# Experts' weights in whole rows over two PSUM banks, with the halves of neighbouring experts interleaved

## The chip, the core and the metric

The kernel runs on one core of a Trainium2 chip. The metric is device time in microseconds (us) from the first to the last instruction of one launch, as the median of several runs. Engines are named as the profile names them: PE multiplies matrices and PEld loads its stationary operand, ACT and DVE work on elements, POOL issues gathers and scatters, SP issues the loads of the weights. The products accumulate in PSUM, which has eight banks of 128 x 512 fp32 here.

## What is computed

Two transformer blocks over 1024 tokens of 1024 channels. The change lies in the experts of the first block. Each of 16 experts takes the 128 tokens that it prefers (twice the 1024 tokens over 16 experts); its three weights have 1024 x 1024 elements in fp32.

```python
def ec_moe(x_tok, w_router, w_gate, w_up, w_down):
    t = x_tok.shape[1]
    cap = CAP_FACTOR * t // N_EXPERTS
    logits = jnp.einsum('btd,de->bte', x_tok, w_router, preferred_element_type=jnp.float32)
    aff = jax.nn.softmax(logits, axis=-1)
    g, idx = lax.top_k(jnp.swapaxes(aff, 1, 2), cap)
    xs = jax.vmap(lambda xt, ix: xt[ix])(x_tok, idx)
    hg = jnp.einsum('becd,edf->becf', xs, w_gate)
    hu = jnp.einsum('becd,edf->becf', xs, w_up)
    y = jnp.einsum('becf,efd->becd', jax.nn.silu(hg) * hu, w_down) * g[..., None].astype(xs.dtype)
    return jax.vmap(lambda ix, val: jnp.zeros((t, D_MODEL), val.dtype)
                    .at[ix.reshape(-1)].add(val.reshape(-1, D_MODEL)))(idx, y)
```

Ahead of the experts stands a mixer of attention and convolution, behind them a second block (`block2`, `final`); neither is touched.

## The kernel before

Every fp32 product is made in three passes. `split` writes an operand as a high part (an ACT cast to fp32r, L82) and a low part (a DVE subtraction, L83), and `mm3` adds high by high, high by low and low by high in one PSUM bank (L77, L78, L79). For a block of weights the parts are `whi` and `wlo`.

The experts run one after another (`moe`, `expert`). For one expert POOL gathers its tokens into `xs` [128 tokens, 1024]; PE transposes them in eight 128 x 128 pieces through two PSUM tiles `tp` (L677), and ACT and DVE split these into `xsh` and `xsl`. Then, for each half `n` of the 1024 columns, `pg` takes the gate product and `pu` the up product; ACT makes `sl = silu(pg)` (L703) and DVE `hh = sl * pu` (L704). The whole `hh` is transposed as `xs` was and split into `hth` and `htl`, which multiply the down weights; the result stands in a tile that is also called `pg`, ACT scales it by the gate into `y` (L711), and POOL scatters `y` with addition into `ff_d` (L712).

The weights come in 192 blocks of 1 MB, twelve to an expert, each [512 rows, 512 columns] (L531), so a DMA reads pieces of 512 elements (2 KB) from rows of 1024. The order is gate, up for the first half of the columns, gate, up for the second, then down; a product of one bank takes two blocks. Three rings set the pace: `raw` has six buffers (`NR`), a load is issued by SP in order as soon as the buffer that it takes is free; `whi` and `wlo` have six more between them and PE (`mw` four, `ml` two). PSUM holds two each of `tp`, `pg` and `pu`, six banks in all. Each engine runs its own instructions in the order that the scheduler of the framework gave them, which the tables of the change show where it matters. PE's work for a block is 12 matmuls 128 x 512 (four row groups, three passes).

Of the kernel before, what the change touches and what calls it, by code (L numbers as in the profile page):

```python
# [44 lines left out]
def rowbc(ap, n=P):  # L45
    """[1, N] row of DRAM read by n partitions."""
    return bass.AP(tensor=ap.tensor, offset=ap.offset, ap=[[0, n], list(ap.ap[-1])])


class Kernel:  # L50
# [34 lines left out]
    def rstd(self, ss, n):  # L85
        """ss <- (ss / n + eps) ** -0.5 by way of ln and exp."""
        self.nc.scalar.activation(ss, ss, AF.Ln, scale=1.0 / n, bias=self.epsc[: ss.shape[0]])
        self.nc.scalar.activation(ss, ss, AF.Exp, scale=-0.5)

    # ---------------------------------------------------------------- constants  # L90
# [39 lines left out]
    # ---------------------------------------------------------------- phase 0  # L130
    def phase0(self):
        """Vectors, the modulation, and the normalised inputs transposed and split."""
        nc, I = self.nc, self.I
        with ExitStack() as st:
# [25 lines left out]
            # silu of c and c_ctx  # L160
# [6 lines left out]
            # lambda  # L167
# [10 lines left out]
            # shift and scale of both streams: a quarter on the vector engine, the rest on the tensor engine  # L178
# [35 lines left out]
            # inputs  # L214
# [26 lines left out]
    # ---------------------------------------------------------------- phase 1  # L241
# [16 lines left out]
    def qkv(self, st):  # L258
        """Queries, keys and values of all heads, split, to DRAM; then the rest of the modulation."""
# [44 lines left out]
    def win(self, c0):  # L304
        """512 columns of the mixer's input projection: (hi, lo) by half of the rows."""
# [13 lines left out]
    # g1 norm_post_mix, sh2, (1 + sc2) norm_pre_ffn, g2 norm_post_ffn  # L319
# [34 lines left out]
    def rope(self, ps, t0, scale, hi, lo):  # L354
        """Rotate the projection in ps (by scale) and split it."""
# [13 lines left out]
    # ---------------------------------------------------------------- attention and convolution  # L369
# [26 lines left out]
    def out_weights(self, w):  # L396
        """The output projection of the mixer, split, where the inputs of its projections were."""
# [13 lines left out]
    def scores(self, i):  # L411
# [19 lines left out]
        # chunk by chunk, each with its own maximum (Q carries -1/8: the least of a row is minus its maximum)  # L431
# [14 lines left out]
    def probs(self, i, E, mx, sm):  # L446
        nc, w, pp = self.nc, self.wp, self.pp
        # weights of the chunks: exp(max of the chunk - max of the row) over the sum of the row
# [76 lines left out]
    # ---------------------------------------------------------------- phase 2  # L525
    def raw512(self, ap, after=None):
        """A [512 rows, 512 columns] block of a weight as it comes, [P, 4, 512]; not before `after` is there."""
        raw = self.t(self.rawp, [P, 4, 512], F32, "raw")
# [5 lines left out]
    def hl512(self, pool, raw, eng=None):  # L534
        hi = self.t(pool, [P, 4, 512], F32R, "whi")
        lo = self.t(pool, [P, 4, 512], F32R, "wlo")
        self.split(raw, hi, lo, eng)
        return hi, lo

    def phase2(self):  # L540
        """Output projection of the mixer, residual, router and the choice of tokens."""
        nc, I = self.nc, self.I
        with ExitStack() as st:
# [4 lines left out]
            for i, r in enumerate((G1, SH2, A2, self.G2)):  # L548
# [5 lines left out]
            self.wblocks = [(n, e, kh, c) for e in range(NE) for n, c, kh in  # L554
                            [(n, c, kh) for c in range(2) for n in ("w_gate", "w_up") for kh in range(2)] + [("w_down", c, kh) for c in range(2) for kh in range(2)]]
# [19 lines left out]
    def next_raw(self, after=None):  # L575
        i = len(self.raws)
        if i < len(self.wblocks):
            n, e, kh, c = self.wblocks[i]
            self.raws.append(self.raw512(self.I[n][0, e, kh * 512:(kh + 1) * 512, c * 512:(c + 1) * 512], after))
# [48 lines left out]
    def choose(self, w, pp, affT):  # L628
        """The CAP largest of each expert: those of either half of the tokens in order, then the better of
        place i of the first half and place CAP - 1 - i of the second."""  # L630
# [28 lines left out]
    # ---------------------------------------------------------------- experts  # L659
    def moe(self):  # L660
        with ExitStack() as st:
            w = self.pool(st, "moe")
            self.ml = self.pool(st, "ml", 2)
            pp = self.pool(st, "moep", 2, space=PSUM)
            for e in range(NE):
                self.expert(e, w, pp)
        self.stx.close()

    def tsplit(self, pp, w, src, nblk, name, bufs=2):
        """src [P rows, nblk*128] transposed in 128-blocks and split: (hi, lo) [P, nblk, P]."""  # L670
# [3 lines left out]
        for k0 in range(0, nblk, 4):  # L674
            tp = self.t(pp, [P, 512], F32, "tp")
# [5 lines left out]
    def block(self):  # L681
        """The next block of the experts' weights, split."""
# [4 lines left out]
        return self.hl512(self.mw if (self.nb - 1) % 6 < 4 else self.ml, raw, self.nc.gpsimd if self.nb <= PB else None)  # L687

    def expert(self, e, w, pp):
        nc, I = self.nc, self.I  # L690

        xs = self.t(w, [P, D], F32, "xs", bufs=2)
        nc.gpsimd.indirect_dma_start(out=xs, out_offset=None, in_=self.xn2_d, in_offset=bass.IndirectOffsetOnAxis(ap=self.idxT[:, e:e + 1], axis=0))
        xh, xl = self.tsplit(pp, w, xs, KB, "xs", bufs=2)
        hh = self.t(w, [P, D], F32, "hh", bufs=1)
        for n in range(2):
            pg = self.t(pp, [P, 512], F32, "pg")
            pu = self.t(pp, [P, 512], F32, "pu")
            for ps in (pg, pu):
                wb = [self.block() for _ in range(2)]  # L700
                self.mm3(ps, [((xh[:, k, :], xl[:, k, :]), (wb[k // 4][0][:, k % 4, :], wb[k // 4][1][:, k % 4, :])) for k in range(KB)])
            sl = self.t(w, [P, 512], F32, "sl", bufs=2)
            self.silu = nc.scalar.activation(sl, pg, AF.Silu)  # L703
            nc.vector.tensor_tensor(hh[:, n * 512:(n + 1) * 512], sl, pu, op=ALU.mult)  # L704
        hT = self.tsplit(pp, w, hh, KB, "ht", bufs=1)
        y = self.t(w, [P, D], F32, "y", bufs=2)
        for n in range(2):
            ps = self.t(pp, [P, 512], F32, "pg")
            wb = [self.block() for _ in range(2)]
            self.mm3(ps, [((hT[0][:, k, :], hT[1][:, k, :]), (wb[k // 4][0][:, k % 4, :], wb[k // 4][1][:, k % 4, :])) for k in range(KB)])  # L710
            nc.scalar.activation(y[:, n * 512:(n + 1) * 512], ps, AF.Copy, scale=self.gT[:, e:e + 1])  # L711
        nc.gpsimd.indirect_dma_start(out=self.ff_d, out_offset=bass.IndirectOffsetOnAxis(ap=self.idxT[:, e:e + 1], axis=0), in_=y, in_offset=None, compute_op=ALU.add)  # L712

    # ---------------------------------------------------------------- second block
# [13 lines left out]
    def ffn_out(self):  # L728
        """Residual of the experts, then the normalised input of the second block, transposed and split."""
# [32 lines left out]
    # projections of the second block, in units of one PSUM tile that fill the tensor engine's gaps  # L762
    def wk(self, c0, n):
        """Columns of the second input projection: [(hi, lo)] by row block."""
# [15 lines left out]
    def fill(self, count=1):  # L780
        """Run the next projection units; the weights of a job come one unit ahead of it."""
# [16 lines left out]
    def chan(self, ws, g, m=P):  # L798
        """[m channels, 512 tokens] of the projection for token group g."""
# [5 lines left out]
    def toks(self, ws, b):  # L805
        """[128 tokens, 2 blocks, 256 channels] of the projection for token blocks b and b + 1."""
# [6 lines left out]
    def logsig(self, w, src, scale, tag, bufs=2):  # L813
        """min(src, 0) - ln(scale + scale exp(-|src|)): the log of the sigmoid, less ln(scale)."""
# [14 lines left out]
    def fox_gate(self, w):  # L829
        """Cumulative log forget gates of the sixteen heads: by head to DRAM, by token on chip."""  # L830
# [22 lines left out]
    # ---- HGRN  # L853
    def hgrn(self):
        nc, I, pp = self.nc, self.I, self.pp
        self.nmm = 3
        with ExitStack() as st:
# [9 lines left out]
            # 1 / (1 - lower bound), the bound from its logits over the one layer  # L867
# [11 lines left out]
            # the work of the heads' projections  # L879
# [585 lines left out]
```

## Time and profile before

| | |
|---|---|
| median of 3 runs | 2911.18 us (2907.66 to 2916.18) |
| span of the profiled execution | 2907.9 us |
| mean granted clock of PE in it, as a share of full speed | 0.966 |
| PE busy over the span | 2656.5 us (91%) |
| DVE busy | 2003.4 us (69%) |
| ACT busy | 1630.0 us (56%) |
| HBM traffic | 177 GB/s over the span |
| the experts' stage, from the first gather to the last scatter | 773 to 1410 us |
| one expert in it | 39.1 us |

The time is the slowest core's, and there is one. The profiled execution's own time is its span, and it lies with the fastest of the three runs; the median is 3.3 us above it. The experts take 22% of the span, and in them alone the DMA queues run at about 350 GB/s, which the page's row of GB/s shows as the stretch of slices from 342 to 336.

### The profile page before, as it was taken

How to read it: one execution, taken by the hardware profiler on the slowest of the kernel's cores; microseconds unless marked ns; L12 is line 12 of the kernel's file. 1: busy time of each engine (PE TensorE's matmuls, PEld its weight loads, DVE VectorE, ACT ScalarE, POOL GpSimd, SP SyncE). 2: the span in 40 equal slices, each digit the busy share in tenths (PEclk: the TensorE clock that was granted, in tenths of full speed). 3: DMA queues.
4: the chain of work that ended last, by engine and by line, in shares of the span. 5: the costliest groups of instructions: out<-in, count | busy, mean ns of one | idle time of the engine just before them, and what ended most of it. 6: DMA issues, size and time to landing. Idle time of an engine off the chain costs nothing.

```text
span 2907.9 us, 38642 instructions
## 1 busy us (share of the span) xinstructions
PE 2656.5 (91%) x14213; PEld 2205.6 (76%) x14213; DVE 2003.4 (69%) x3287; ACT 1630.0 (56%) x2858; POOL 278.1 (10%) x344
## 2 busy tenths in 40 slices
PE   7899999887699999999499999999999998989998
PEld 3677887776577777777489999998878787767776
DVE  5864999845777778777447777674677776786435
ACT  4212898733366667766445555453566665674335
POOL 0101000003011011110010000000111111231000
PEclk8999999998799999999799999999999999999999
DMA  8666333256499999999621112314665666475712
GB/s 279 216 211 195 94 89 90 79 182 238 148 342 351 351 359 345 347 347 336 203 74 38 37 52 44 44 52 127 185 172 160 147 166 137 134 199 178 215 59 80
DMA packets 358242, 516.43 MB, mean 178 GB/s; under 512 B 52529, under 2 KB 180094, under 8 KB 358052
## 3 DMA queue, kind: packets, MB, share of 16 engines
q1 hardware_dynamic: 340780, 456.04, 51.1%
q0 software_dynamic: 11136, 36.25, 4.2%
q10 hardware_dynamic: 6136, 21.67, 2.0%
q8 instruction: 112, 1.84, 0.3%
q14 instruction: 78, 0.64, 0.1%
HBM read 421.01 MB, written 92.88 MB: 177 GB/s over the span
## 4 chain that ended last, share of the span: by engine, by line
PE 53%; DMA 7%; ACT 6%; DVE 4%; issue 3%; SPq 0%; POOL 0%; DVEq 0%; ACTq 0%; POOLq 0%
PE mm L77 9%; PE mm L79 9%; PE mm L78 9%; PE pg L79 4%; PE pg L77 4%; PE pg L78 4%; PE av L1266 2%; PE sc L987 2%; PE pu L79 2%; PE pu L77 2%; PE pu L78 2%; ACT whi L82 1%; DVE wlo L83 1%; PE tp L1257 1%; PE sc L1228 1%
## 5 line engine op out<-in xcount | busy, mean ns | idle before, releaser
L83 DVE TENSOR_TENSOR wlo<-raw,whi 128x2048 fp32r<-128x2048 f32 (+1 forms) x280 | 546.3, 1965 | 237.5 <-ACT whi L82 234.3
L82 ACT CAST whi<-raw 128x2048 fp32r<-128x2048 f32 (+1 forms) x284 | 465.1, 1647 | 236.4 <-PE pg L79 96.9
L77 PE MATMUL mm<-uh,whi 128*128 128x512 f32 x640 | 259.6, 406 | 0.9 <-ACT uh L759 0.9
L78 PE MATMUL mm<-ul,whi 128*128 128x512 f32 x640 | 256.7, 401 | 0.0
L79 PE MATMUL mm<-uh,wlo 128*128 128x512 f32 x640 | 256.5, 401 | 0.0
L79 PE MATMUL mm<-whi,ul 128*128 128x256 f32 x768 | 220.2, 287 | 0.0
L77 PE MATMUL mm<-whi,uh 128*128 128x256 f32 x768 | 220.2, 287 | 0.0
L78 PE MATMUL mm<-wlo,uh 128*128 128x256 f32 x768 | 217.8, 284 | 0.0
L79 PEld LDWEIGHTS mm<-whi,ul 128*128 128x128 f32 x768 | 145.4, 189 | 0.1
L77 PEld LDWEIGHTS mm<-whi,uh 128*128 128x128 f32 x768 | 145.3, 189 | 0.2
L78 PEld LDWEIGHTS mm<-wlo,uh 128*128 128x128 f32 x768 | 145.1, 189 | 0.2
L1235 ACT ACTIVATE lg<-lg,sm 128x128 f32<-128x128 f32 (+7 forms) x128 | 99.5, 777 | 81.5 <-DVE sm L1234 81.0
L79 PEld LDWEIGHTS mm<-uh,wlo 128*128 128x128 f32 x640 | 122.5, 191 | 26.4
L77 PEld LDWEIGHTS mm<-uh,whi 128*128 128x128 f32 x640 | 122.5, 192 | 24.9 <-ACT uh L759 1.4
L78 PEld LDWEIGHTS mm<-ul,whi 128*128 128x128 f32 x640 | 122.5, 191 | 23.9
L442 ACT ACTIVATE e<-sc,mx 128x512 f32<-128x512 f32 (+1 forms) x192 | 118.1, 625 | 39.0 <-DVE mx L441 37.8
L77 PE MATMUL mm<-xh,whi 128*128 128x512 f32 x320 | 128.6, 402 | 5.6 <-DVE stl L83 4.2
L79 PE MATMUL mm<-xh,wlo 128*128 128x512 f32 x320 | 127.3, 398 | 0.0
L78 PE MATMUL mm<-xl,whi 128*128 128x512 f32 x320 | 126.9, 397 | 0.0
L1266 PE MATMUL av<-pT,V 128*128 128x256 f32 x640 | 108.9, 299 | 17.0 <-ACT pT L82 12.4
L1266 PEld LDWEIGHTS av<-pT,V 128*128 128x128 f32 x640 | 91.9, 196 | 41.1 <-ACT pT L82 29.8
L1231 DVE SCALAR_TENSOR_TENSOR lg<-sc,FT,nF 128x512 f32<-128x512 f32 (+3 forms) x160 | 91.6, 582 | 39.0 <-PE sc L1228 28.1
(386 smaller groups left out, 7041.4 us busy)
## 6 DMA issues: line engine op xcount, KB each, us to landing
raw<-in_w_gate_dram SPq DMA_DIRECT2D x64, 1024.0 KB
raw<-in_w_up_dram SPq DMA_DIRECT2D x64, 1024.0 KB
raw<-in_w_down_dram SPq DMA_DIRECT2D x64, 1024.0 KB
raw<-in_w_in_dram SPq DMA_DIRECT2D x76, 512.0 KB
wada<-in_w_ada_dram SPq DMA_DIRECT2D x32, 512.0 KB
Q<-Q_d SPq DMA_DIRECT2D x64, 256.0 KB
yraw<-yT_d SPq DMA_DIRECT2D x22, 512.0 KB
raw<-in_w_ada_dram SPq DMA_DIRECT2D x8, 1024.0 KB
```

The lines of the kernel that those rows point to most:

```text
L77: self.nc.tensor.matmul(ps, ah, bh, start=(i == 0), stop=False)
L78: self.nc.tensor.matmul(ps, ah, bl, start=False, stop=False)
L79: self.nc.tensor.matmul(ps, al, bh, start=False, stop=(i == n - 1))
L82: self.nc.scalar.copy(hi, src)
L83: (eng or self.nc.vector).tensor_tensor(lo, src, f(hi), op=ALU.subtract)
L442: nc.scalar.activation(e[:, c0:c0 + n], ps[:, :n], AF.Exp, scale=-1.0, bias=mx[:, m, c:c + 1], accum_out=sm[:, m, c:c + 1])
L987: nc.tensor.matmul(pair(ps, c), kl[:, c * P:(c + 1) * P], pair(ql, c), start=True, stop=True)
L1228: nc.tensor.matmul(ps[:, :mm], Q[j][:, tb * P:(tb + 1) * P], K[:, c0:c0 + mm], start=(j == 0), stop=(j == 1))
L1231: nc.vector.scalar_tensor_tensor(lg[:, c0:c0 + full], ps[:, :full], Ft, nF[:, c0:c0 + full], op0=ALU.subtract, op1=ALU.add)
L1235: nc.scalar.activation(lg[:, :n], lg[:, :n], AF.Exp, scale=-1.0, bias=sm[:, 0:1], accum_out=sm[:, 1:2])
L1257: nc.tensor.transpose(tp[:, k * P:(k + 1) * P], lg[:, (k0 + k) * P:(k0 + k + 1) * P], self.ident)
L1266: nc.tensor.matmul(ps[:, :256], V[:, k, :], pT[k // 4][j][:, k % 4, :], start=(k + j == 0), stop=(k == nkb - 1 and j == 1))
```

## The change

A block is now 256 whole rows (`rawrows`), one piece of 1 MB in DRAM, which the DMA reads in pieces of 1024 elements (4 KB). There are still twelve blocks to an expert and 12 matmuls to a block, but a product takes four blocks (`q` 0 to 3), and each block feeds two banks, one for each half of the columns (`rows`): the tiles are `pg0`, `pg1`, `pu0`, `pu1`, and for the down product `py0`, `py1` of their own, one buffer each, which with two `tp` makes all eight banks.

The order of the products interleaves neighbouring experts. Iteration `e` runs the first block of gate of expert `e`, the transposes of `hh` of expert `e-1`, the other three blocks of gate and the first two of up, the gather and the transposes of `xs` of expert `e+1` (`chosen`), the last two blocks of up, the down product of `e-1`, then `silu` and `hh` of `e` and last `y` and its scatter for `e-1` (`combine`). `wblocks` lists the loads in the same order. `hh` has two buffers instead of one. The numbers of instructions of each kind and shape stay as they were, and nothing of the program behind or ahead of the experts changes but the place of two loads of later weights (128 x 4 x 256) in SP's order.

```diff
-            self.wblocks = [(n, e, kh, c) for e in range(NE) for n, c, kh in
-                            [(n, c, kh) for c in range(2) for n in ("w_gate", "w_up") for kh in range(2)] + [("w_down", c, kh) for c in range(2) for kh in range(2)]]
+            self.wblocks = []
+            for e in range(NE + 1):
+                if e < NE:
+                    self.wblocks += [(n, e, q) for n in ("w_gate", "w_up") for q in range(4)]
+                if e:
+                    self.wblocks += [("w_down", e - 1, q) for q in range(4)]
...
-            self.raws.append(self.raw512(self.I[n][0, e, kh * 512:(kh + 1) * 512, c * 512:(c + 1) * 512], after))
+            self.raws.append(self.rawrows(self.I[n][0, e, q * 256:(q + 1) * 256, :], after))
...
-            pp = self.pool(st, "moep", 2, space=PSUM)
-            for e in range(NE):
-                self.expert(e, w, pp)
+            pp = self.pool(st, "moep", 1, space=PSUM)
+            xs = self.chosen(0, w, pp)
+            hh = None
+            for e in range(NE + 1):
+                hT = None
+                if e < NE:
+                    pg = [self.t(pp, [P, 512], F32, f"pg{n}") for n in range(2)]
+                    pu = [self.t(pp, [P, 512], F32, f"pu{n}") for n in range(2)]
+                    self.rows(pg, xs, 0)
+                if e:
+                    hT = self.tsplit(pp, w, hh, KB, "ht", bufs=1)
+                if e < NE:
+                    for q in range(1, 4):
+                        self.rows(pg, xs, q)
+                    for q in range(2):
+                        self.rows(pu, xs, q)
+                    nxt = self.chosen(e + 1, w, pp) if e + 1 < NE else None
+                    for q in range(2, 4):
+                        self.rows(pu, xs, q)
+                    xs = nxt
+                if e:
+                    py = [self.t(pp, [P, 512], F32, f"py{n}") for n in range(2)]
+                    for q in range(4):
+                        self.rows(py, hT, q)
+                if e < NE:
+                    hh = self.t(w, [P, D], F32, "hh", bufs=2)
+                    for n in range(2):
+                        sl = self.t(w, [P, 512], F32, "sl", bufs=2)
+                        self.silu = self.nc.scalar.activation(sl, pg[n], AF.Silu)
+                        self.nc.vector.tensor_tensor(hh[:, n * 512:(n + 1) * 512], sl, pu[n], op=ALU.mult)
+                if e:
+                    self.combine(e - 1, w, py)
...
+    def rows(self, ps, x, q):
+        hi, lo = self.block()
+        xh, xl = x
+        for k in range(2):
+            i = q * 2 + k
+            for n in range(2):
+                c = slice(n * 512, (n + 1) * 512)
+                self.nc.tensor.matmul(ps[n], xh[:, i, :], hi[:, k, c], start=(i == 0), stop=False)
+                self.nc.tensor.matmul(ps[n], xh[:, i, :], lo[:, k, c], start=False, stop=False)
+                self.nc.tensor.matmul(ps[n], xl[:, i, :], hi[:, k, c], start=False, stop=(i == KB - 1))
```

The scheduler turns this into an order for each engine. The first place is PE, before, where an expert's up product ends and its down product begins (a name is a tile and its number; `hh` is the expert's hidden layer).

```order
L78 MATMUL pu_9057<-wlo_9103,xsh_8962 128x512
L79 MATMUL pu_9057<-whi_9102,xsl_8963 128x512
L677 MATMUL tp_9135<-ident_59,hh_8978 128x128 x4
L677 MATMUL tp_9142<-ident_59,hh_8978 128x128 x4
L77 MATMUL pg_9150<-whi_9153,hth_9133 128x512
L78 MATMUL pg_9150<-wlo_9154,hth_9133 128x512
L77 MATMUL pg_9188<-whi_9191,hth_9133 128x512
```

The same transposes in the change, for ten of the fifteen experts that have another behind them: they stand inside the down product of the expert before (its tiles are `py`, its hidden layer `hth_10241`). For the other five they stand between gate's first block and its second, as the code is written.

```order
L733 MATMUL py_2012_10402<-whi_10405,htl_10242 128x512
L731 MATMUL py_2011_10401<-whi_10423,hth_10241 128x512
L731 MATMUL py_2012_10402<-whi_10423,hth_10241 128x512
L711 MATMUL tp_10510<-ident_59,hh_10475 128x128 x4
L711 MATMUL tp_10517<-ident_59,hh_10475 128x128 x3
L732 MATMUL py_2011_10401<-wlo_10424,hth_10241 128x512
L733 MATMUL py_2011_10401<-whi_10423,htl_10242 128x512
```

What moved: the transposes stood alone between `hh` and the first product with `hth`, and now have matmuls that do not need them on both sides. The second place is PE in the change where a down product (`py`) has ended and gate goes on, in the same ten: the last matmuls with gate's first block (`whi_10225`), then the transposes of the expert after next's `xs`, and the first matmuls with gate's second block (`whi_10259`, `wlo_10260`).

```order
L732 MATMUL pg_1975_10220<-wlo_10226,xsh_10082 128x512
L733 MATMUL pg_1975_10220<-whi_10225,xsl_10083 128x512
L711 MATMUL tp_10351<-ident_59,xs_10347 128x128 x3
L731 MATMUL pg_1974_10219<-whi_10259,xsh_10082 128x512
L731 MATMUL pg_1975_10220<-whi_10259,xsh_10082 128x512
L711 MATMUL tp_10351<-ident_59,xs_10347 128x128
L711 MATMUL tp_10358<-ident_59,xs_10347 128x128 x4
L732 MATMUL pg_1974_10219<-wlo_10260,xsh_10082 128x512
```

Before, the next expert's gate also followed at once on the down product, behind the transposes of its own `xs`; now it has one block of 12 matmuls ahead of those. The third place is ACT, before, over the down product of one expert: each `y` half stands between casts of weights.

```order
L82 CAST hth_9667<-tp_9669 128x512
L82 CAST hth_9667<-tp_9676 128x512
L82 CAST whi_9820<-raw_9691 128x2048
L711 ACTIVATE y_9683<-pg_9684,gT_5637 128x512
L82 CAST whi_9826<-raw_9723 128x2048
L82 CAST whi_9861<-raw_9729 128x2048
L711 ACTIVATE y_9683<-pg_9722,gT_5637 128x512
L82 CAST xsh_9763<-tp_9765 128x512
```

ACT in the change at one of the ten: `whi_9658` is the last block of a down product, `whi_9691` gate's first block of the expert after, `whi_9725` its second.

```order
L82 CAST whi_9658<-raw_9564 128x2048
L82 CAST whi_9691<-raw_9582 128x2048
L745 ACTIVATE y_9681<-py_1846_9600,gT_5637 128x512
L82 CAST hth_9707<-tp_9709 128x512
L745 ACTIVATE y_9681<-py_1847_9601,gT_5637 128x512
L82 CAST hth_9707<-tp_9716 128x512
L82 CAST whi_9725<-raw_9602 128x2048
```

ACT in the change at one of the five: `whi_7555`, `whi_7589`, `whi_7607` and `whi_7625` are gate's four blocks and `whi_7643` is up's first, and both halves of `y` come behind all of them.

```order
L82 CAST whi_7555<-raw_7446 128x2048
L82 CAST whi_7589<-raw_7466 128x2048
L82 CAST whi_7607<-raw_7484 128x2048
L82 CAST whi_7625<-raw_7502 128x2048
L82 CAST whi_7643<-raw_7520 128x2048
L745 ACTIVATE y_7545<-py_1406_7464,gT_5637 128x512
L745 ACTIVATE y_7545<-py_1407_7465,gT_5637 128x512
```

What moved: both halves of `y` now wait for the end of a down product at one place of ACT's order, and at the ten they stand ahead of the cast of gate's second block, with the two casts of `hth`.

## Rows read from the trace of the kernel before

**Rows 1.** The page: busy time of each engine, and GB/s in 40 slices.
```profile
PE 2656.5 (91%) x14213; PEld 2205.6 (76%) x14213; DVE 2003.4 (69%) x3287; ACT 1630.0 (56%) x2858; POOL 278.1 (10%) x344
...
GB/s 279 216 211 195 94 89 90 79 182 238 148 342 351 351 359 345 347 347 336 203 74 38 37 52 44 44 52 127 185 172 160 147 166 137 134 199 178 215 59 80
```

**Rows 2.** Windows, one expert each: span, busy PE PEld DVE ACT POOL, clock, DMA, GB/s.
```profile
881.00:920.10 39.10, 35.81 (x162) 28.55 (x161) 30.62 (x19) 26.88 (x21) 5.36 (x2) 1.00 1.00 348
...
959.20:998.30 39.10, 35.81 (x162) 28.60 (x161) 30.65 (x19) 26.91 (x21) 5.37 (x2) 1.00 1.00 351
```

**Rows 3.** Waits, 800 to 1420: who for whom, us in total, times, longest.
```profile
DVE wlo L83 <- ACT whi L82: 135.8, 94, 5.3
ACT whi L82 <- PE pg L79: 93.3, 46, 4.2
ACT whi L82 <- PE pu L79: 32.6, 45, 0.9
...
PE tp L677 <- DVE hh L704: 24.0, 15, 1.7
...
PE pg L79 <- DVE htl L83: 17.0, 14, 1.2
...
PE pg L77 <- ACT xsh L82: 5.7, 15, 0.4
...
PE pg L77 <- ACT hth L82: 2.0, 1, 2.0
```

**Rows 4.** Waits of SP's queue, 800 to 1420.
```profile
SPq L531 <- DVE wlo L83: 495.8, 177, 7.1
```

**Rows 5.** PE's timeline at the start of a down product: start, us, operation, idle before.
```profile
885.79 0.66 PE L677 MATMUL tp<-ident,hh 128*128 128x128 f32 x4 [1.69 <-DVE hh L704]
...
888.60 0.50 PE L79 MATMUL pg<-whi,htl 128*128 128x512 f32 x1 [1.22 <-DVE htl L83]
888.94 0.39 PE L77 MATMUL pg<-whi,hth 128*128 128x512 f32 x1
```

**Rows 6.** PE's timeline from a down product to the next expert's gate.
```profile
898.83 1.03 PE L677 MATMUL tp<-ident,xs 128*128 128x128 f32 x8
900.24 0.50 PE L77 MATMUL pg<-whi,xsh 128*128 128x512 f32 x1 [0.38 <-ACT xsh L82]
900.58 0.39 PE L78 MATMUL pg<-wlo,xsh 128*128 128x512 f32 x1
900.80 0.40 PE L77 MATMUL pu<-whi,xsh 128*128 128x512 f32 x1
```

**Rows 7.** Groups by line and shape, 780 to 1420: busy us, mean ns, idle before.
```profile
L83 DVE TENSOR_TENSOR wlo<-raw,whi 128x2048 fp32r<-128x2048 f32 x186 | 421.9, 2289 | 132.1 <-ACT whi L82 132.0
L82 ACT CAST whi<-raw 128x2048 fp32r<-128x2048 f32 x186 | 352.3, 1908 | 130.0 <-PE pg L79 96.9 <-PE pu L79 32.6 <-issue 0.5
...
L711 ACT ACTIVATE y<-pg,gT 128x512 f32<-128x512 f32 x32 | 22.0, 688 | 24.6 <-PE pg L79 24.6
...
L82 ACT CAST hth<-tp 128x512 fp32r<-128x512 f32 x32 | 18.7, 583 | 9.5 <-PE tp L677 9.5
```

**Rows 8.** DMA over one expert (881 to 920.1): packets, and GB/s in 40 slices.
```profile
GB/s 381 390 388 383 388 386 390 386 388 390 386 386 390 386 243 57 132 400 409 166 344 409 407 337 254 272 260 224 268 398 409 406 402 398 379 396 383 390 383 388
DMA packets 6605, 13.61 MB, mean 348 GB/s; under 512 B 224, under 2 KB 224, under 8 KB 6603
```

**Rows 9.** Windows with weights alone, then with pieces of 4 KB (`h`, `ff`); columns as Rows 2.
```profile
876.00:892.00 16.00, 13.09 (x61) 10.23 (x60) 12.48 (x8) 9.37 (x8) 0.00 (x0) 1.00 1.05 387
1434.00:1446.00 12.00, 3.67 (x12) 2.79 (x12) 7.60 (x9) 9.82 (x26) 2.06 (x4) 0.50 1.03 420
```

**Rows 10.** Timeline of PE and ACT at the last expert's end.
```profile
1404.36 0.39 PE L79 MATMUL pg<-whi,htl 128*128 128x512 f32 x1
...
1406.52 1.04 ACT L82 CAST whi<-raw 128x1024 fp32r<-128x1024 f32 x1 [2.75 <-DMA raw<-in_w_in_dram]
1407.47 0.68 ACT L711 ACTIVATE y<-pg,gT 128x512 f32<-128x512 f32 x1
```

More of the change, by code (lines that the diff above doesn't have):

```diff
@@ L523, in conv, with rawrows @@
             self.store(self.mixT_d[512 + cb * P:512 + (cb + 1) * P, :], y)
-    def raw512(self, ap, after=None):
-        raw = self.t(self.rawp, [P, 4, 512], F32, "raw")
+    def rawrows(self, ap, after=None):
+        raw = self.t(self.rawp, [P, 2, D], F32, "raw")
         if after is not None:
@@ L532, in raw512, with hlrows @@
         return raw
-    def hl512(self, pool, raw, eng=None):
-        hi = self.t(pool, [P, 4, 512], F32R, "whi")
-        lo = self.t(pool, [P, 4, 512], F32R, "wlo")
+    def hlrows(self, pool, raw, eng=None):
+        hi = self.t(pool, [P, 2, D], F32R, "whi")
+        lo = self.t(pool, [P, 2, D], F32R, "wlo")
         self.split(raw, hi, lo, eng)
@@ L577, in next_raw @@
         if i < len(self.wblocks):
-            n, e, kh, c = self.wblocks[i]
-            self.raws.append(self.raw512(self.I[n][0, e, kh * 512:(kh + 1) * 512, c * 512:(c + 1) * 512], after))
+            n, e, q = self.wblocks[i]
+            self.raws.append(self.rawrows(self.I[n][0, e, q * 256:(q + 1) * 256, :], after))
     def mixed(self, w, pp, tb, wo, G1, SH2, A2, wr, af):
@@ L674, in tsplit @@
         for k0 in range(0, nblk, 4):
-            tp = self.t(pp, [P, 512], F32, "tp")
+            tp = self.t(pp, [P, 512], F32, "tp", bufs=2)
             for k in range(4):
@@ L686, in block @@
             self.next_raw()
-        return self.hl512(self.mw if (self.nb - 1) % 6 < 4 else self.ml, raw, self.nc.gpsimd if self.nb <= PB else None)
-    def expert(self, e, w, pp):
-        nc, I = self.nc, self.I
-        xs = self.t(w, [P, D], F32, "xs", bufs=2)
[L693 to L705, printed above, removed]
+        return self.hlrows(self.mw if (self.nb - 1) % 6 < 4 else self.ml, raw, self.nc.gpsimd if self.nb <= PB else None)
@@ L706, in expert, with chosen, combine @@
+    def chosen(self, e, w, pp):
+        xs = self.t(w, [P, D], F32, "xs", bufs=2)
+        self.nc.gpsimd.indirect_dma_start(out=xs, out_offset=None, in_=self.xn2_d, in_offset=bass.IndirectOffsetOnAxis(ap=self.idxT[:, e:e + 1], axis=0))
+        return self.tsplit(pp, w, xs, KB, "xs", bufs=2)
+    def combine(self, e, w, py):
         y = self.t(w, [P, D], F32, "y", bufs=2)
         for n in range(2):
-            ps = self.t(pp, [P, 512], F32, "pg")
-            wb = [self.block() for _ in range(2)]
@@ L710, in expert @@
-            self.mm3(ps, [((hT[0][:, k, :], hT[1][:, k, :]), (wb[k // 4][0][:, k % 4, :], wb[k // 4][1][:, k % 4, :])) for k in range(KB)])
-            nc.scalar.activation(y[:, n * 512:(n + 1) * 512], ps, AF.Copy, scale=self.gT[:, e:e + 1])
-        nc.gpsimd.indirect_dma_start(out=self.ff_d, out_offset=bass.IndirectOffsetOnAxis(ap=self.idxT[:, e:e + 1], axis=0), in_=y, in_offset=None, compute_op=ALU.add)
+            self.nc.scalar.activation(y[:, n * 512:(n + 1) * 512], py[n], AF.Copy, scale=self.gT[:, e:e + 1])
@@ L715, in block2 @@
+        self.nc.gpsimd.indirect_dma_start(out=self.ff_d, out_offset=bass.IndirectOffsetOnAxis(ap=self.idxT[:, e:e + 1], axis=0), in_=y, in_offset=None, compute_op=ALU.add)
     def block2(self):
```

## The prediction

> **What bounds the kernel now.** I read the page first: PE is busy for 91% of the span, DVE for 69%, ACT for 56%, and the DMA queues come near a full load only in the experts' stage [rows 1]. So the stage has two candidates, PE and DMA, and I looked at single experts. The windows of one expert are alike to a hundredth: 39.10 us, PE busy for 35.81 of them at full clock, DVE 30.6, ACT 26.9, and a DMA share of 1.00 [rows 2]. PE is idle for 3.29 us in each; that, and little more, is there to be taken from PE.
>
> The waits tell PE and DMA apart. If the loads were late, ACT's casts would wait for `raw` and PE for `whi` or `wlo`. Neither stands in the list for the weights. ACT's casts wait for PE to free a buffer (93.3 and 32.6 us), and DVE for ACT [rows 3]. SP's queue, which issues the loads, waits for DVE to free a `raw` buffer 177 times for 495.8 us [rows 4]: the queues are full because requests stand in them early, not because PE needs the data. PE's own waits are four, all of them on small steps inside one expert: transposes of `hh` for DVE (24.0), the first product with `htl` for DVE (17.0), the first with `xsh` for ACT (5.7), and one on `hth` (2.0); together 48.7 us [rows 3].
>
> The timelines show where. Down begins only when `hh` is made, transposed and split: 1.69 us idle ahead of the second four transposes, 1.22 ahead of `htl` [rows 5]; between two experts 0.38 us for `xsh` [rows 6]. Each wait costs something behind it too: matmuls start 0.22 to 0.23 us apart, but the second after a wait starts 0.34 after the first [rows 5, 6]. That is 0.1 us for each, three to an expert.
>
> **The change part by part.** *Removed.* The transposes of `hh` get an unrelated product on both sides, and so do those of `xs`. DVE then has at least 12 matmuls (2.8 us) for `hh` and its split, against the 1.69 and 1.22 us that it was late. All 48.7 us of waits go, and 15 x 3 x 0.1 = 4.5 us of slow starts: -53.2 us. Without the cover it would be nothing.
>
> *Added.* A single tile per bank and both halves of a product ending together put the two `y` at one place of ACT's order. At the ten late boundaries ACT then has `y`, `hth`, `y`, `hth` and the cast of gate's second block, and it can't begin before the first `py` is done. From the groups [rows 7]: 0.69 + 0.58 + 0.69 + 0.58 + 1.91 = 4.45 us until `whi`, and 2.29 more until `wlo`. PE meanwhile has three matmuls of the other `py` (0.69), twelve of gate's first block (12 x 0.23 = 2.77) and three transposes (3/8 of 1.03 = 0.39 [rows 6]): 3.85 us. It waits 0.6 us for `whi`. Two matmuls and five transposes later (0.46 + 0.64 = 1.10) it waits for `wlo`, 2.29 - 1.10 = 1.2 us. That is 1.8, and with two slow starts 2.0: ten times, +20 us. The bounds: 0 if ACT's short steps overlap or the scheduler's order leaves slack, and 6.7 each (4.45 + 2.29) if gate's first block is no cover. I take the sum, since every term but the transposes' share has its row. Queued behind the `y` on ACT are only the casts, and who waits for these is PE. At the five other boundaries ACT's order has four more casts ahead of the `y`, so PE has four blocks (11 us) in hand, and I add nothing.
>
> *Pieces of 4 KB.* Weights alone come at 387 GB/s in pieces of 2 KB, and where the queues carry pieces of 4 KB I read 420 [rows 9]. A block of 1.0486 MB would take 2.50 us in place of 2.71, twelve of them 2.5 us less. By the waits this is worth nothing today, because PE waits for no load; it becomes the cover for a shorter period. How much DMA an expert needs is not shown, since the queue empties at times: slices of 57, 132 and 166 GB/s, others of 224 to 272 while tokens are gathered and scattered [rows 8]. From below, twelve blocks at 2.71 and 1.05 MB of gather and scatter at the same rate make 13.61 MB at 387 = 35.2 us, so 32.7 after; from above the whole 39.10, so 36.6 after. PE's new period is 39.10 - 53.2/15 = 35.55 us at the five boundaries and 37.55 at the ten, 36.9 in the mean: covered even by the upper bound, but narrowly. At 2 KB the upper bound would not be covered.
>
> The Trainium skill (Perfetto Trace Analysis, DMA Optimizations) calls batching 2 KB pieces into 4 KB or 8 KB the primary optimization when a kernel is DMA-bound. The waits say that this one is not [rows 3, 4]; were it so, the saving would be 16 x 2.5 = 40 us in place of my sum.
>
> *At nothing.* The counts of matmuls, transposes, casts and bytes stay, so PE's work is 35.8 us in each. Matmuls that alternate between two banks keep their pace already: `pg` and `pu` at 0.22 us [rows 6]. POOL's gather comes earlier in an expert, and POOL is free for 34 us of 39 [rows 2]. Two loads of later weights move in SP's order, and their casts come far behind.
>
> *The end.* The last `y` is cast 2.7 us after PE's last matmul (1404.36 + 0.39 = 1404.75 to 1407.47), behind a cast that waits for its load [rows 10]. Both halves now stand at the end and ahead of that cast, but two of them, 0.6 more: -2.1 us.
>
> **Sum.** -53.2 + 20.0 - 2.1 = -35.3 us. The profiled span of 2907.9 becomes 2872.6. The median of before lies 3.3 us above its span, and I keep this: 2876 us.
>
> **The rivals.** *No new wait.* Everything is removed and ACT's short steps cost nothing: 2911.2 - 55.3 = 2856. For it: a step on ACT starts 0.1 us before the one ahead of it is over [rows 10]. Against it: `wlo` alone (2.29) is longer than the 1.10 us of cover behind `whi`.
>
> *DMA becomes the bound.* Today its share is 1.00 [rows 2]. If the pieces give only half of what I take, an expert needs up to 39.10 - 1.25 = 37.85 us; 15 x 1.25 + 2.1 = 21 us gained: 2890. For it: the queue is full nearly all the time. Against it: the slices under 170 GB/s are time to spare, and data wait for ACT, not ACT for data.
>
> The Trainium skill (DMA: Bandwidth & Descriptors, Specifications) puts a core's HBM limit at about 358 GB/s. By it 13.61 MB take 38.0 us, an estimate from that page, which would give 2911 - 17 - 2 = 2892. The trace shows 387 and 420 GB/s, above it [rows 9].
>
> *The change does not do what it says.* The DMA is the bound already and stays at 348 to 351 GB/s [rows 2]: 2911 or a little less. Against it are the 495.8 us that SP waits for buffers [rows 4].
>
> *Slower.* ACT's queue is the mechanism: if gate's first block is not split when a down product ends, nothing covers the chain, and PE waits for all of 6.7 us at each late boundary: 67 - 55.3 = +12, 2923. It decides from 5.5 us (55.3/10) on. For it: ACT must cast that block one place ahead of the `y`. Against it: its `whi` buffer is the one of up's third block, free five blocks (14 us) before.
>
> **How the numbers follow.** My forecast has 0.57, no new wait 0.16, DMA as the bound 0.17, no change 0.06, slower 0.04. A measurement tells about 0.3%, 9 us, from no change. The first three lie over that: 0.90 less a little for a weaker DMA, 0.89 faster, 0.07 same, 0.04 slower. The range of 2855 to 2895 takes in the first three with their bounds, 0.9 of the chance on paper and rather 0.8 with the terms that no row shows; the forecast's own is 2866 to 2884, which is a new wait of 0.9 to 2.7 us at each of the ten.
>
> **What would show it right or wrong.** Right: no waits of PE for `hh` or `htl`; a wait of 0.6 us for `whi` and 1.2 for `wlo` at gate's second block, at ten boundaries and not at five; periods of 35.5 and 37.5 us; windows of weights above 400 GB/s with a DMA share under 1. Wrong: casts that wait for `raw` (DMA is the bound), PE waiting for `wlo` at other blocks than gate's second, or matmuls more than 0.23 us apart.

## The result, and the profile after

The changed kernel takes 2870.3 us in the median (2866.5 to 2874.7, four runs) against 2913.5 for the kernel before beside it; the ratio is 0.9859, with a 95% interval of 0.9846 to 0.9872. That is 43 us less where 35 were forecast, inside the range. In a second measurement (e8 below) the ratio was 0.9864 (0.9849 to 0.9879).

Where it came from is read first from four points on PE: the first transposes of `xs`, the last matmul of the experts, the first `mm` of the second block, the end. The timeline of PE before, at the first and the third:

```profile
781.62 1.94 PE L677 MATMUL tp<-ident,xs 128*128 128x128 f32 x8 [9.61 <-DMA xs<-xn_d,idxT]
...
1446.17 0.80 PE L77 MATMUL mm<-uh,whi 128*128 128x512 f32 x1 [0.35 <-ACT uh L759]
```

And after, at the first, the second (with the last `y` on ACT) and the third:

```profile
775.41 1.94 PE L711 MATMUL tp<-ident,xs 128*128 128x128 f32 x8 [9.93 <-DMA xs<-xn_d,idxT]
...
1359.64 1.37 ACT L745 ACTIVATE y<-py,gT 128x512 f32<-128x512 f32 x2 [6.22 <-PE py L733]
1359.89 0.39 PE L733 MATMUL py<-whi,htl 128*128 128x512 f32 x1
...
1397.24 0.80 PE L77 MATMUL mm<-uh,whi 128*128 128x512 f32 x1 [0.35 <-ACT uh L793]
```

With the last matmul of before at 1404.36 [rows 10], the experts' stage went from 622.74 us to 584.48 (-38.3), and the stretch behind it from 41.81 to 37.35 (-4.5). What lies ahead was 6.2 us shorter and what lies behind 5.7 longer in this pair of executions; that is code which the change does not touch, and in the runs below, with the same code there, the first point lies anywhere from 775.3 to 782.2.

The windows of one expert after (columns as [rows 2]), an early one and two late ones:

```profile
941.67:976.70 35.03, 35.03 (x161) 28.72 (x160) 28.27 (x17) 24.55 (x19) 2.63 (x2) 1.00 1.00 359
1049.59:1086.57 36.98, 35.62 (x161) 28.67 (x160) 30.56 (x18) 26.36 (x21) 3.14 (x2) 1.00 1.01 376
1086.57:1123.54 36.97, 35.62 (x161) 28.68 (x160) 30.56 (x18) 26.16 (x21) 3.14 (x2) 1.00 1.01 371
```

In the early one PE is busy for the whole 35.03 us: there is no gap left. The late ones last 1.94 us longer, with 1.36 idle. The first `y` starts of two experts that follow each other are 35.03 us apart four times, then 35.92 once, eight times 36.97 and at last 37.42. The two odd ones:

```profile
976.70:1012.62 35.92, 35.92 (x169) 29.43 (x168) 28.27 (x17) 24.56 (x20) 2.64 (x2) 1.00 0.98 359
...
1308.37:1345.79 37.42, 35.03 (x153) 27.62 (x152) 29.36 (x16) 26.57 (x19) 1.55 (x1) 1.00 0.88 316
```

The first has eight matmuls more than the others (169 in place of 161) and no idle time, the second eight fewer (153): where the order changes, the eight transposes of a second `hh` come into the one, and in the other there is no further `xs` to transpose. The waits after, 770 to 1420 (who for whom, us in total, times, longest):

```profile
ACT y L745 <- PE py L733: 99.1, 16, 8.8
...
PE pg L732 <- DVE wlo L83: 10.0, 9, 1.6
...
ACT whi L82 <- DMA raw<-in_w_gate_dram: 5.1, 8, 1.0
...
ACT whi L82 <- DMA raw<-in_w_down_dram: 3.9, 6, 0.8
...
PE pg L731 <- ACT whi L82: 3.1, 9, 0.6
...
PE py L732 <- DVE wlo L83: 1.5, 1, 1.5
```

Of the four waits of [rows 3], 48.7 us, three are gone, and the one on `hth` is down to 0.6 us, once. New are the two that were forecast, on `whi` and `wlo` of gate, nine times each, 13.1 us. Before the last down product, which no gate follows, PE waits once more for `wlo`, 1.5 us. PE's timeline at one of the nine:

```profile
1089.86 0.49 PE L711 MATMUL tp<-ident,xs 128*128 128x128 f32 x3
1090.65 0.73 PE L731 MATMUL pg<-whi,xsh 128*128 128x512 f32 x2 [0.31 <-ACT whi L82]
1091.22 0.71 PE L711 MATMUL tp<-ident,xs 128*128 128x128 f32 x5
1092.98 0.50 PE L732 MATMUL pg<-wlo,xsh 128*128 128x512 f32 x1 [1.05 <-DVE wlo L83]
```

And ACT's, at the same place:

```profile
1086.57 0.69 ACT L745 ACTIVATE y<-py,gT 128x512 f32<-128x512 f32 x1 [7.57 <-PE py L733]
1087.16 0.58 ACT L82 CAST hth<-tp 128x512 fp32r<-128x512 f32 x1
1087.62 0.71 ACT L745 ACTIVATE y<-py,gT 128x512 f32<-128x512 f32 x1
1088.20 0.60 ACT L82 CAST hth<-tp 128x512 fp32r<-128x512 f32 x1
1088.67 3.74 ACT L82 CAST whi<-raw 128x2048 fp32r<-128x2048 f32 x2
```

The reader sees the chain of the prediction step by step: ACT stands idle for 7.57 us until the first `py` is done, then five steps follow on each other, and PE gets its `whi` 4.0 us after the first `y` began. The DMA over the same expert, GB/s in 40 slices and packets:

```profile
GB/s 412 328 390 425 346 164 155 204 168 425 394 421 417 412 417 412 421 412 421 425 381 399 417 372 306 403 368 403 417 421 421 425 288 390 403 386 403 386 284 390
DMA packets 3569, 13.71 MB, mean 371 GB/s; under 512 B 225, under 2 KB 225, under 8 KB 3568
```

About the same bytes in little more than half the packets of [rows 8] (3569 against 6605), and slices of 412 to 425 GB/s where weights alone had 380 to 390.

### The profile page after: what moved, and what is told of

Its sections match the earlier page's. It is cut to its first block, busy times and chain, and to the rows that moved or that the text cites. A ratio compares the mean times of both kernels' runs of the same rounds, so it can differ in the third digit from the quotient of the medians.

```text
span 2864.7 us, 38667 instructions
## 1 busy us (share of the span) xinstructions
PE 2645.4 (92%) x14213; PEld 2205.3 (77%) x14213; DVE 2002.0 (70%) x3287; ACT 1624.9 (57%) x2858; POOL 247.7 (9%) x344
## 4 chain that ended last, share of the span: by engine, by line
PE 54%; DMA 7%; ACT 6%; DVE 3%; issue 2%; SPq 0%; POOL 0%; DVEq 0%; ACTq 0%; POOLq 0%
PE mm L77 9%; PE mm L79 9%; PE mm L78 9%; PE av L1300 2%; PE pu L732 2%; PE pu L733 2%; PE pu L731 2%; PE pg L732 2%; PE py L732 2%; PE py L733 2%; PE py L731 2%; PE pg L733 2%; PE pg L731 2%; PE sc L1021 2%; PE tp L1291 1%
## 5 line engine op out<-in xcount | busy, mean ns | idle before, releaser
L442 ACT ACTIVATE e<-sc,mx 128x512 f32<-128x512 f32 (+1 forms) x192 | 118.3, 626 | 39.1 <-DVE mx L441 38.2
L1265 DVE SCALAR_TENSOR_TENSOR lg<-sc,FT,nF 128x512 f32<-128x512 f32 (+3 forms) x160 | 91.7, 583 | 40.5 <-PE sc L1262 28.1
```

The source lines that it names most:

```text
L442: nc.scalar.activation(e[:, c0:c0 + n], ps[:, :n], AF.Exp, scale=-1.0, bias=mx[:, m, c:c + 1], accum_out=sm[:, m, c:c + 1])
L1265: nc.vector.scalar_tensor_tensor(lg[:, c0:c0 + full], ps[:, :full], Ft, nF[:, c0:c0 + full], op0=ALU.subtract, op1=ALU.add)
```

## The experiments

My theory: the order of the products brought the gain, because it takes PE's small waits away; the pieces of 4 KB are at most a cover; and ACT's order costs about 2 us at each late boundary. The main rival: the pieces brought it. Twelve blocks of 0.21 us, fifteen times, are 38 us, just what the stage lost, so the sum alone can't tell the two apart.

The stage lengths below are from the first transposes of `xs` to the start of the last matmul of the experts, as above, in one profiled execution of each; one expert is the time from one first `y` to the next, without the places where the order changes (35.9 and 37.4 in e2 and e8, 37.3 and 35.3 in e3 and e4, 41.7 in e5 and e6, 37.3 to 39.6 three times in e7) and the last experts; the kernel before beside e1 to e4 had a median of 2908.4 us, beside e5 to e8 of 2910.3.

| run | order | pieces | stage, us | one expert, us | median, us | ratio to before (95%) |
|---|---|---|---|---|---|---|
| before | one by one | 2 KB | 622.7 | 39.10 | 2908.4, 2910.3 | 1 |
| e1 | one by one | 4 KB | 634.6 | 39.6 to 40.5 | 2920.1 | 1.0040 (1.0028 to 1.0053) |
| e2 | interleaved | 2 KB | 584.5 | 35.03, 36.9 to 37.0 | 2871.4 | 0.9867 (0.9848 to 0.9886) |
| e8, the change | interleaved | 4 KB | 584.5 | 35.03, 36.97 | 2869.6 | 0.9864 (0.9849 to 0.9879) |
| e3 | `y` later | 4 KB | 576.5 | 35.03, 36.2 | 2863.1 | 0.9848 (0.9832 to 0.9864) |
| e4 | `y` later | 2 KB | 577.6 | 35.03, 36.2 | 2861.1 | 0.9837 (0.9822 to 0.9853) |
| e5 | early for all | 4 KB | 567.8 | 35.03 | 2851.3 | 0.9790 (0.9773 to 0.9806) |
| e6 | early for all | 2 KB | 573.3 | 35.03 to 37.26 | 2855.2 | 0.9817 (0.9802 to 0.9832) |
| e7 | e5, `xs` in the gap | 4 KB | 580.3 | 35.71 | 2865.4 | 0.9853 (0.9839 to 0.9866) |

**e1: whole rows, experts one by one.** `wblocks` and `moe` without the interleaving; `rows` stays.

```diff
-            for e in range(NE + 1):
-                if e < NE:
-                    self.wblocks += [(n, e, q) for n in ("w_gate", "w_up") for q in range(4)]
-                if e:
-                    self.wblocks += [("w_down", e - 1, q) for q in range(4)]
+            for e in range(NE):
+                self.wblocks += [(n, e, q) for n in ("w_gate", "w_up", "w_down") for q in range(4)]
...
+            for e in range(NE):
+                xs = self.chosen(e, w, pp)
...
+                for ps in (pg, pu):
                     for q in range(4):
+                        self.rows(ps, xs, q)
...
+                hT = self.tsplit(pp, w, hh, KB, "ht", bufs=1)
...
+                for q in range(4):
+                    self.rows(py, hT, q)
+                self.combine(e, w, py)
```

> One part of the change alone: whole rows of 4 KB over two banks, but each expert is finished before the next begins. If the order of the products brought the gain (my theory), PE keeps its waits for hh, htl and xsh at every expert, about 4 us of an expert's 39: within 10 us of the kernel before, 2903 to 2923. If the larger pieces brought it (rival: 12 blocks of 0.21 us less, 15 times, is 38 us), the time is 2870 to 2880.

It is slower than before by 0.4%, and the stage by 11.8 us. The larger pieces and the two banks bring nothing without the new order. PE's waits of e1, 770 to 1420:

```profile
PE tp L694 <- DVE hh L678: 29.6, 14, 2.1
...
PE pg L714 <- ACT xsh L82: 5.7, 15, 0.4
PE py L716 <- DVE htl L83: 3.9, 5, 0.9
```

Both halves of up now end together, so `hh` is later than before: 2.1 us in place of 1.7. All eight transposes of `hh` now stand behind this wait, where before four stood ahead of it [rows 5]. The windows of two experts in it show something else besides, in the clock's column (the third from the end):

```profile
1094.74:1134.98 40.24, 37.67 (x161) 29.60 (x160) 30.92 (x19) 27.38 (x20) 2.98 (x2) 0.96 0.91 339
1134.98:1174.64 39.66, 36.22 (x161) 28.63 (x160) 30.93 (x19) 27.40 (x21) 2.98 (x2) 1.00 0.92 346
```

It comes back below. The DMA share is 0.90 to 0.93 in every expert of e1: with 4 KB the same bytes need less time, and nothing uses it.

**e2: the change's order, pieces of 2 KB.** The two halves of a row go to different places of the tile, so a piece is half a row.

```diff
-        raw = self.t(self.rawp, [P, 2, D], F32, "raw")
+        raw = self.t(self.rawp, [P, 2, 2, 512], F32, "raw")
...
-        self.nc.sync.dma_start(raw, ap.rearrange("(k p) c -> p k c", p=P))
+        self.nc.sync.dma_start(raw, ap.rearrange("(k p) (n c) -> p n k c", p=P, n=2))
...
```

> The other part alone: the changed kernel's order and banks, but each block of 256 rows is read in pieces of 2 KB (half a row each) as before. If the order brought the gain, at least half of the 43 us stays: 2868 to 2890, the upper end if the DMA at 2 KB can no longer keep up with 37 us for an expert (then ACT waits for raw). If the pieces brought it, nothing is left: 2905 to 2915.

The stage is that of the changed kernel to a tenth, 584.5 us. A late window, and PE's main wait in e2:

```profile
1126.18:1163.16 36.98, 35.62 (x161) 28.68 (x160) 30.57 (x18) 26.38 (x21) 3.14 (x2) 1.00 1.03 370
```
```profile
PE pg L731 <- DVE wlo L83: 10.0, 9, 1.6
```

The same wait, the same nine times. The pieces give nothing at this period, and the rival falls. e1 and the changed kernel have the same pieces and banks and differ in the order: 50 us of the stage (634.6 against 584.5). The order over the old blocks of one bank was not run. Even at 2 KB the DMA keeps up with 37 us.

**e3 and e4: `y` later on ACT.** `combine` of an expert moves into the next expert's gate, tied behind the cast of the second block; e4 has pieces of 2 KB as e2.

```diff
+                        if q == 1 and done:
+                            with self.tc.issue_after(self.cast.ins):
+                                self.combine(done[0], w, done[1])
...
-                    self.combine(e - 1, w, py)
+                    done = (e - 1, py)
```

> The changed kernel with y and its scatter issued in the next expert's gate, on ACT behind the cast of gate's second block. If ACT's order alone makes PE wait at the nine boundaries that last 37 us (my theory), each falls to 35.0: 15 to 19 us less than the changed kernel, 2851 to 2856. If the DMA already limits those periods (rival: its share there is 1.00 to 1.01), the wait only moves to the casts of raw: 2864 to 2872.

> The same with pieces of 2 KB. If the larger pieces are the cover for the shorter period, as I forecast, PE loses it here: periods of 36 to 39 us with casts that wait for raw, 2870 to 2900. If the DMA has room at 2 KB as well, 2851 to 2858.

Less than half of what I had expected: the late periods fall from 36.97 to 36.2, not to 35.0. The reason is neither of the two that I had named. PE's wait at gate is gone, and another has come (e3, 770 to 1420):

```profile
PE pu L741 <- DVE wlo L83: 8.4, 10, 0.9
```

ACT's timeline over a late period of e3 shows what is behind it:

```profile
1123.82 1.07 ACT L82 CAST hth<-tp 128x512 fp32r<-128x512 f32 x2 [4.87 <-PE py L741]
...
1135.32 0.60 ACT L705 ACTIVATE sl<-pg 128x512 f32<-128x512 f32 x1 [1.91 <-PE pg L742]
1135.81 1.90 ACT L82 CAST whi<-raw 128x2048 fp32r<-128x2048 f32 x1
```

ACT still waits in its queue: `hth` has one buffer, so its cast can't begin before the down product that reads it is over, and the transposes inside that product win nothing; then `sl` waits 1.91 us for the end of gate, with the cast of up's next block behind it. That e4 has the same periods at 2 KB rules the DMA out as the cause.

**e5 and e6: the early order for all experts.** The order of the first five periods is forced on the rest: the transposes are tied behind matmuls on PE, `y` and `silu` behind casts on ACT. (`y` still moves back once against it, by 6.7 us, and stays there.) e6 has pieces of 2 KB.

```diff
+                    with self.tc.issue_after(self.last.ins):
+                        hT = self.tsplit(pp, w, hh, KB, "ht", bufs=1)
...
+                        if q == 3 and done:
+                            with self.tc.issue_after(self.cast.ins):
+                                self.combine(done[0], w, done[1])
...
+                    with self.tc.issue_after(self.last.ins):
+                        nxt = self.chosen(e + 1, w, pp) if e + 1 < NE else None
...
+                    with self.tc.issue_after(mark if e else self.cast.ins):
```

Here `self.last` is the matmul issued last, `self.cast` the last cast of a block, and `mark` the cast of down's first block, behind which `silu` follows.

> The changed kernel with the order of its first five periods kept for all: the transposes of hh right behind gate's first block and those of xs behind up's second (so neither lies in a down product), y on ACT behind the cast of gate's fourth block, silu behind that of down's first. If only the order of ACT made the later periods 37 us (my theory), all fourteen are 35.0 us and the time is 15 to 19 us under the changed kernel, 2849 to 2855 where the changed kernel has 2867 to 2871. If the DMA limits (rival: the queues are full, 13.61 MB in 35.03 us are 389 GB/s), periods come out at 36 us or more with casts that wait for raw and PE waiting for whi or wlo: 2858 to 2870.

> The same with pieces of 2 KB, the hardest test of the forecast that the larger pieces are the cover. If they are, periods lie over 35.0 us here: 13.61 MB at the 387 GB/s of weights alone are 35.2, and more with the gathers, so 36 or more and 2860 to 2885. If 2 KB have room even at 35.0, the time is that of e5 within 3 us, and the pieces do nothing in this kernel.

e5 is the fastest version: 2851.3 us (2842.2 to 2853.6) beside 2869.6 (2868.6 to 2871.3) for the changed kernel on the same chip, 18 us less, and 2.1% under the kernel before. Windows of e5 from the middle of the stage and from near its end:

```profile
1025.58:1060.62 35.04, 35.04 (x161) 28.71 (x160) 30.56 (x18) 26.14 (x22) 3.30 (x2) 1.00 1.02 389
...
1270.82:1305.85 35.03, 35.03 (x161) 28.71 (x160) 30.56 (x18) 25.91 (x22) 2.32 (x1) 1.00 1.02 377
```

No gap on PE in either, and the DMA moves 389 GB/s over a whole expert. So ACT's and PE's order alone made the late boundaries. In e6 the first periods are as short, the later ones are not:

```profile
1056.09:1091.13 35.04, 35.04 (x161) 28.71 (x160) 30.82 (x18) 26.49 (x22) 3.31 (x2) 1.00 1.05 377
1126.81:1162.64 35.83, 35.27 (x161) 28.62 (x160) 30.56 (x18) 26.88 (x21) 4.63 (x2) 1.00 1.05 377
1198.74:1236.00 37.26, 36.34 (x164) 28.91 (x163) 30.64 (x19) 26.76 (x21) 5.10 (x2) 1.00 1.05 377
```

The waits of e6, 770 to 1420:

```profile
ACT whi L82 <- DMA raw<-in_w_gate_dram: 24.5, 29, 2.1
ACT whi L82 <- DMA raw<-in_w_down_dram: 23.6, 22, 2.1
ACT whi L82 <- DMA raw<-in_w_up_dram: 20.5, 18, 2.3
```

ACT waits 68.6 us for weights, 69 times; in e5 it is 7.3 us. This is what a DMA bound looks like in these views: a rate that stays at 377 GB/s whatever the period, then casts that wait, and periods that grow. 13.61 MB at 377 are 36.1 us, an estimate of what an expert needs at 2 KB, between my bounds of 35.2 and 39.1. In the changed kernel (36.97 us) it is covered; in e5 it would not be, and there the pieces of 4 KB are worth 5.5 us of the stage, and 3.9 in the medians.

**e7: one wait put back.** e5 with `chosen` behind the down product, so that the transposes of `xs` stand in the gap between two experts.

```diff
-                    with self.tc.issue_after(self.last.ins):
-                        nxt = self.chosen(e + 1, w, pp) if e + 1 < NE else None
...
+                if e + 1 < NE:
+                    with self.tc.issue_after(self.last.ins):
+                        xs = self.chosen(e + 1, w, pp)
```

> e5 with the transposes of the next expert's xs put back between the down product and that expert's gate, where the kernel before has them: one wait of 0.3 to 0.4 us for xsh in each of 15 experts, and nothing else. By the forecast's price of a wait (its idle time and 0.1 us of a slow start) the period is 35.03 + 0.48 = 35.5 and the time 7 us over e5. If a wait costs PE 0.27 us beyond its idle time (the rival price, from the 4.07 us an expert that went with 3.25 us of waits), the period is 35.7 and the time 10 us over e5.

A window, and PE's timeline at the gap in it:

```profile
1131.25:1166.95 35.70, 35.46 (x161) 28.64 (x160) 30.47 (x19) 26.37 (x22) 2.73 (x2) 1.00 1.02 382
```
```profile
1160.78 1.03 PE L723 MATMUL tp<-ident,xs 128*128 128x128 f32 x8
1162.05 0.50 PE L743 MATMUL pg<-whi,xsh 128*128 128x512 f32 x1 [0.24 <-ACT xsh L82]
...
1164.96 1.04 PE L723 MATMUL tp<-ident,hh 128*128 128x128 f32 x8
```

PE shows 0.24 us idle, but the period is 0.67 longer than in e5. The eight transposes of `xs` take 1.27 us from their start to the next matmul's, those of `hh`, with no wait, 0.79: 0.48 for a wait of 0.24. So a wait costs 0.24 beyond its idle time, near the rival price of 0.27 and not the forecast's 0.1. That the period meets the 35.7 of the rival is in part luck: the wait was 0.24 and not the 0.38 expected. The rest of the 0.67 shows no idle time: 0.10 is a slow start inside the down product (1152.76 to 1153.09, 0.33 us from one matmul to the next), and the last 0.1 stands at no single place. The time is 14 us over e5, 12.5 in the stage; 14 periods of 0.67 make 9.4. The other 3 us lie at the stage's two ends and in three early periods in which the scheduler mixed another order, and were not taken apart.

**e8: the changed kernel again.**

> The changed kernel itself, on the same chip as e5 to e7, for their differences: 2867 to 2873.

2869.6 us (2868.6 to 2871.3), as expected.

## Why the prediction was right, and where its sizes were off

*What is removed.* The mechanism held: PE's waits inside an expert went, and e1, which keeps them, keeps the time. The size was too small: an expert without late boundary takes 35.03 us, not 35.55. The mis-sized term is "15 x 3 x 0.1 = 4.5 us of slow starts". A wait costs more beyond its idle time than the one slow start that I read, and the 35.8 us that I took as PE's fixed work have it in them. Matmuls start 0.23 us apart but are booked for 0.39 each [rows 5], so the last 0.16 us of the one ahead of a wait count as busy though nothing else runs. Three lines of before, beside those in [rows 5], give the starts:

```profile
883.51 0.60 PE L677 MATMUL tp<-ident,hh 128*128 128x128 f32 x4
...
886.21 0.48 PE L77 MATMUL pg<-whi,hth 128*128 128x512 f32 x1
...
886.98 0.40 PE L78 MATMUL pg<-wlo,hth 128*128 128x512 f32 x1
```

From 883.51 to 886.21 are 2.70 us, where eight transposes without a wait take 0.79 (e7): 1.91 for 1.69 shown. From 886.98 to 888.94 are 1.96, where two matmuls take 0.46: 1.50 for 1.22. In [rows 6] it is 0.64 for 0.38. That is 0.22 to 0.28 more for each, 4.05 us for an expert in place of 3.55; the periods say 4.07. Over the 14 periods between the first and the last pair of `y` it makes -57.0 us.

*What is added.* Forecast 2.0 us at ten boundaries. Eight measured 1.94. The two odd periods add 0.9 and 2.4, which is the ninth: the 0.9 are the eight transposes that moved, and the ninth boundary has no transposes of `xs` to cover the wait. That makes 18.8 us; the tenth, ahead of the last down product, lies behind the last pair of `y` counted here. That 2.0 came so near 1.94 is in part luck, since its parts were off both ways. The waits shown are 0.31 and 1.05 in place of 0.6 and 1.2: ACT's steps overlap by 0.1 us each (4.0 us until `whi` is there, not 4.45), and the two matmuls and five transposes ahead of the wait for `wlo` take 1.28, not 1.10. What lies beyond the idle time is 0.58, not 0.2, the same mis-sized price. -57.0 + 18.8 = -38.2 is the stage's -38.3. That the order on the engines makes the late boundaries is shown by e5, where they are gone with every product and byte kept. The prediction took the two `y` for what waits there. e3 moves only these, and 0.77 of the 1.94 goes: the casts of `hth` wait at the same place for the end of the same down product, which the prediction counted with their length only.

*Pieces of 4 KB.* "Worth nothing today" was right: e2. "At 2 KB the upper bound would not be covered" was the bound's word; the need is 36.1 us by the estimate from e6, so 2 KB were enough at 37 us and not at 35. The sign named for it, a DMA share under 1, was a wrong sign: SP issues a load whenever a buffer comes free, so the queues stay full (1.01) in a kernel whose DMA has time to spare; e1, with 39.6 us and more for an expert, shows 0.90 to 0.93. SP's waits for a buffer [rows 4], which I held against a DMA bound, don't tell it either: from 800 to 1340 they are 465 us before and still 410 in e6. The sign "casts that wait for `raw`" showed in the changed kernel with 14 waits, 9.0 us, and in e2 with 13.5, both at the same stage length; in e6 it is 68.6 and the periods grow. So it is their amount, with the period, that tells.

The Trainium skill (Perfetto Trace Analysis, DMA Optimizations) ranks the step from 2 KB to 4 KB first for a DMA-bound kernel; e5 against e6 agrees, 5.5 us of the stage, and e2 shows that it is nothing where the bound lies elsewhere. Its limit of about 358 GB/s for a core (DMA: Bandwidth & Descriptors, Specifications) is passed in e5 with 389 GB/s over 35 us.

*The end.* Forecast -2.1, measured -4.5 in this pair: the last `y` began 0.25 us ahead of the start of PE's last matmul instead of 3.1 behind it, which makes 2.7 with the second half; where the rest comes from stays open.

*The sum.* The three terms were off by 3.8, 1.2 and 2.4 us, all to the same side, so the forecast's 35 is not near 43 by cancelling. One step of the arithmetic was off by 0.1: the 2866 to 2884 of the forecast are a new wait of 1.0 to 2.8 us, not 0.9 to 2.7.

*The rivals.* "No new wait" did not happen in the change, but e5 is near that case: 2851 where 2856 were worked out for it. "DMA becomes the bound" is e6, not the change. "Slower" named ACT's queue, where the new waits do come from, but its price of 6.7 us was never near: 1.94 was measured.

## What to carry to other kernels

Work that lets the busiest engine go on during a short dependent step is worth what that step costs from start to start, not only the idle time that the list of waits shows; add about 0.25 us here for each wait of PE (0.22 to 0.28 measured). When steps are gathered at one place of an engine's order (here two `y` and two casts ahead of the block that PE needs next), look at that order, not only at the code: tying a few instructions behind others gave another 18 us on top of the change's 43. A full DMA queue is no sign of a DMA bound by itself, nor are loads that wait for buffers a sign against it; try the smaller pieces, and see whether the engines wait more for data and the period grows.

## What the hardware showed that I had not expected

In e1 the granted clock of PE fell to near the lower of its two levels for about three microseconds, after it had run matmuls for 24 us with a single idle time of 0.38 us and then stood idle for 2.12 us. Windows of e1 just before, at and after such a place (columns as [rows 2]):

```profile
1078.00:1081.30 3.30, 1.47 (x7) 0.85 (x5) 2.81 (x3) 2.40 (x2) 0.00 (x0) 1.00 1.02 408
1081.30:1084.50 3.20, 2.91 (x11) 2.50 (x12) 3.20 (x4) 1.28 (x3) 0.00 (x0) 0.54 1.03 410
...
1088.00:1092.00 4.00, 4.00 (x19) 3.30 (x18) 2.37 (x2) 3.02 (x2) 0.00 (x0) 1.00 0.30 115
```

And PE's transposes there, and two experts on, where the clock stayed at 1.00:

```profile
1081.59 1.97 PE L694 MATMUL tp<-ident,hh 128*128 128x128 f32 x8 [2.12 <-DVE hh L678]
...
1161.47 1.26 PE L694 MATMUL tp<-ident,hh 128*128 128x128 f32 x8 [2.12 <-DVE hh L678]
```

The clock is 0.54 in the second window (1.2 GHz is one half), and the eight transposes take 1.97 us there in place of 1.26. Of twelve experts of e1 in a row, eight have a mean clock of 0.96 and four one of 1.00. The idle time shown is 2.12 us at both places above, and why the clock did not fall at the second stays open. Before, with an idle time of 1.69, the clock stayed at 1.00 [rows 2].

What this adds to e1 can be read off its periods. The four at a clock of 1.00 last 39.60 to 39.66 us, half a microsecond over the 39.10 of before; fifteen such make some 8 of the 11.8 us by which the stage is longer. That part goes with the later `hh` and the eight transposes behind it, and the other 4, in the longer periods, with the clock (an estimate from these periods, not measured apart). The eight at 0.96 last 39.63 to 40.45, so a fallen clock cost up to 0.8 us for an expert, and at two of the eight, with 39.63, nothing.
